# Weight pairs of two projections asked for by ScalarE behind a cast, in place of SyncE behind a gemv load

## The chip, the cores and the metric

The kernel runs on one core of a Trainium2 chip. A core has TensorE (PE in the profile; its weight loads are listed as PEld), VectorE (DVE), ScalarE (ACT), GpSimd (POOL) and SyncE (SP), each with a queue of instructions of its own that it works through in order. They share an on-chip memory (SBUF, 128 partitions) and the matmul banks (PSUM, eight banks of 128 x 512 floats). Data come from the chip's main memory by DMA: an engine's queue asks for a transfer, and 16 DMA engines move it. The metric is the device time of one execution in microseconds (us), lower is better.

## The reference

One decoder block on 512 tokens of width 2048, all in float32:

```python
mod = silu(c) @ w_ada + b_ada                      # six vectors of 2048
shift1, scale1, gate1, shift2, scale2, gate2 = split(mod, 6)
h = rms_norm(x, norm1_w) * (1 + scale1) + shift1
proj = h @ w_in                                    # 2048 x 7168
aq, ak, av, gq, gf, gi, gg = split(proj, ...)      # 1024 columns each
attn = rms_norm(dilated_attention(rope(rms_norm(aq)), rope(rms_norm(ak)), av), attn_out_norm_w)
hg = rms_norm(hgrn2(gq, gf, gi), hg_norm_w) * silu(gg)
x = x + gate1 * (concat([attn, hg]) @ w_out)       # 2048 x 2048
h2 = rms_norm(x, norm2_w) * (1 + scale2) + shift2
x = x + gate2 * (square(relu(h2 @ w_ff1)) @ w_ff2) # 2048 x 8192 x 2048
```

The attention has 8 heads of 128 with three dilated windows, merged by their softmax denominators; `hgrn2` is a gated linear recurrence with 8 heads of 128.

## The kernel before

**Split operands.** Every large product is made of three matmuls. An operand is split into a rounded part `hi` and a rest `lo = x - hi`, and `hi*hi + hi*lo + lo*hi` is summed in a bank. For weights this is `_split` (line 35): ScalarE casts the loaded tile to `whi` (line 39), and VectorE subtracts to get `wlo` (line 40). Both tiles have four buffers, so the cast of a row block waits until TensorE is done with the row block four places back.

**Loading weights.** `load_w` (line 188) loads a *pair*: two row blocks of 128 x 512, 512 KB in one DMA, into a tile `wraw` with four buffers, and splits both. A buffer is free when both casts and both splits of the pair four places back are done. The DMA is asked for on SyncE's queue (line 192). `load_w` runs under `tc.high_priority()`, which lets the planner place these instructions ahead of others.

**The projections.** `project` (line 371) makes 512 columns of `proj`: four banks, eight pairs, and for each row block twelve matmuls by `tok_mm` (lines 201 to 203) or `ch_mm` (209 to 211). After each row block it takes steps of other work: `tick()` advances the attention and recurrence tasks, `bg_step()` the gemv work. It is called eleven times after the first two column groups, which `first_groups` makes. `project_out` (line 877) makes 512 columns of the output projection in the same way and is called four times. Between two calls ScalarE copies the four banks out (lines 410, 570, 711, 944), since the next call needs banks too.

**The gemv.** The six modulation vectors are products of a single row, made on VectorE: `gemv` (line 118) loads `w_ada` piece by piece into `araw` (four buffers, 256 KB each, line 125, on SyncE's queue), and VectorE multiplies and adds (lines 129 and 131). `asked[0]` keeps the last such load. The results go through TensorE transposes (lines 151 and 182) and ScalarE (line 154).

**The order.** From line 849 on, the order of TensorE's instructions is the order in which the program is written. The order on the other engines and on SyncE's queue is set beforehand by a planner, which simulates the kernel with its own durations and priorities. `tc.issue_after(ins)` makes the instructions in its block come after `ins` on the same engine, without waiting for its end. In `project`, `marks` keeps for each pair the gemv load that was last asked for, and from the fourth pair on a weight pair comes behind the gemv load noted three pairs before. `project_out` has no such order.

**After the projections**, the feed-forward layer uses `load_w` without an order (lines 975 and 1013) and then larger weight tiles (line 1155) on SyncE's queue.

Of the kernel before, what the change touches and what calls it, by code (L numbers as in the profile page):

```python
# [34 lines left out]
def _split(nc, pool, src, n=512, eng=None):  # L35

    hi = pool.tile([P, 512], F32R, name="whi", tag="whi")[:, 0:n]
    lo = pool.tile([P, 512], F32R, name="wlo", tag="wlo")[:, 0:n]
    nc.scalar.copy(hi, src)  # L39
    (eng or nc.vector).tensor_tensor(lo, src, hi.bitcast(F32), op=ALU.subtract)  # L40
    return hi, lo

# [2 lines left out]
def hybrid_block(ctx, tc, x, c, positions, norm1_w, w_ada, b_ada, w_in, q_norm_w, k_norm_w,  # L45
                 attn_out_norm_w, hg_lb_logits, hg_norm_w, w_out, norm2_w, w_ff1, w_ff2,
                 lnc, hgmask, inv_freq, out):
    nc = tc.nc
    pe, dve, act, pool = nc.tensor, nc.vector, nc.scalar, nc.gpsimd
# [4 lines left out]
    win_v = w_in[0].rearrange("(k p) n -> p k n", p=P)  # L54
    wout_v = w_out[0].rearrange("(k p) n -> p k n", p=P)
# [5 lines left out]
    wr = pw.enter_context(tc.tile_pool(name="wr", bufs=4))  # L61
# [6 lines left out]
    def bank(name, tag="bg"):  # L68
        return ps.tile([P, 512], F32, name=name, tag=tag)
# [43 lines left out]
    pool.dma_start(ifq, inv_freq.broadcast_to([P, 16]))  # L113


    asked, marks = [None], []

    def gemv(view, vec, col0, n=512, early=False):

        accs = [(work("acc") if early else gv.tile([P, 512], F32, name="acc"))[:, 0:n] for _ in range(2)]  # L120
        nk = 512 // n
        for k0 in range(0, NK, nk):
            raw = spare.pop(0) if early and spare else slot("araw") if early else gv.tile([P, 512], F32, name="araw", bufs=4)
            raw = raw.rearrange("p (k n) -> p k n", n=n)
            asked[0] = nc.sync.dma_start(raw, view[:, k0:k0 + nk, col0:col0 + n])
            for k in range(k0, k0 + nk):
                acc = accs[k % 2]
                if k < 2:
                    dve.tensor_scalar(acc, raw[:, k - k0], vec[:, k:k + 1], None, op0=ALU.mult)
                else:  # L130
                    dve.scalar_tensor_tensor(acc, raw[:, k - k0], vec[:, k:k + 1], acc, op0=ALU.mult, op1=ALU.add)  # L131
            yield
        gemv.acc = accs
# [28 lines left out]
    def mod_cols(kind, b, dst, nw, n=512, early=False):  # L162

        for _ in gemv(ada_v, sc, kind * D + b * n, n, early):
            yield
        nb = n // P
        d = dst[:, b * nb:(b + 1) * nb]
        yield from to_cols(gemv.acc, d)
        dve.tensor_tensor(d, d, bcol[:, kind * NK + b * nb:kind * NK + (b + 1) * nb], op=ALU.add)
        if nw is not None:  # L170
            mod_cols.last = dve.scalar_tensor_tensor(d, d, 1.0, nw[:, b * nb:(b + 1) * nb], op0=ALU.add, op1=ALU.mult)
        yield
# [15 lines left out]
    def load_w(view, k0, c0, n=512, eng=None, ahead=True, raws=None, behind=False):  # L188
        with tc.high_priority() if ahead else ExitStack():
            raw = wr.tile([P, 2, n], F32, name="wraw", tag="raw", bufs=4)  # L190
            with tc.issue_after(marks[-3].ins) if behind else ExitStack():
                nc.sync.dma_start(raw, view[:, k0:k0 + 2, c0:c0 + n])
            if raws is not None:
                raws[:] = [raw[:, 0], raw[:, 1]]
            return [_split(nc, wr, raw[:, j], n, eng if j else None) for j in range(2)]

    def tok_mm(banks, hi, lo, whi, wlo, first, last):

        for ti in range(NT):
            ts = slice(ti * P, (ti + 1) * P)  # L200
            pe.matmul(banks[ti], lhsT=hi[:, ts], rhs=whi, start=first, stop=False)  # L201
            pe.matmul(banks[ti], lhsT=hi[:, ts], rhs=wlo, start=False, stop=False)  # L202
            pe.matmul(banks[ti], lhsT=lo[:, ts], rhs=whi, start=False, stop=last)  # L203
# [27 lines left out]
    def slot(name, dt=F32):  # L231
        return io.tile([P, 512], dt, name=name, tag="io")

    def work(name, dt=F32):
        return wk.tile([P, 512], dt, name=name, tag="wk")
# [55 lines left out]
    def first_groups(c_f, c_q, before, after):  # L291

        bt = [bank("prj", tag="mm") for _ in range(4)]
        bc = [bank("prc") for _ in range(2)]
        for k0 in range(0, NK, 2):
            before(k0)
            wt = load_w(win_v, k0, c_f, ahead=False)
            wc = load_w(win_v, k0, c_q, 256, None, ahead=False)
            for j in range(2):
                k = k0 + j  # L300
                ch_mm(bt, hhi[k], hlo[k], *wt[j], k == 0, k == NK - 1)
                ch_mm(bc, hhi[k], hlo[k], *wc[j], k == 0, k == NK - 1)
            after(k0)
        return bt, bc
# [14 lines left out]
    shift_done, behind = set(), []  # L319
# [29 lines left out]
    def bg_step():  # L349

        while bgw:
            try:
                return next(bgw[0])
            except StopIteration:
                bgw.pop(0)
# [3 lines left out]
    def tick(n=1):  # L359

        for _ in range(n):
            while tasks:
                try:
                    next(tasks[0])
                    break
                except StopIteration:
                    tasks.pop(0)
# [3 lines left out]
    def project(c0, mm, rate=1.85, after=None):  # L371

        banks = [bank("prj", tag="mm") for _ in range(4)]
        for k0 in range(0, NK, 2):
            for j, (whi, wlo) in enumerate(load_w(win_v, k0, c0, 512, None, behind=len(marks) > 2)):
                k = k0 + j
                mm(banks, hhi[k], hlo[k], whi, wlo, k == 0, k == NK - 1)
                tick()
                owed[0] += rate
                while owed[0] >= 1.0:  # L380
                    bg_step()
                    owed[0] -= 1.0
                if after:
                    after(k)
            marks.append(asked[0])
        return banks

    mix = [None] * NK
# [1 line left out]
    korder = list(range(8, 12)) + list(range(8)) + list(range(12, 16))  # L390

    def split_mix():

        if len(mixp) == NK or mix[korder[len(mixp)]] is None:
            return False
        mixp.append(pair(len(mixp)))
        split_to(mixp[-1], mix[korder[len(mixp) - 1]])
        return True
# [43 lines left out]
    def qk(c0, name, i):  # L442
        ts = evac(project(c0, tok_mm), name)
        rs = sm.tile([P, NT, 4], F32, name=f"rs{i}", bufs=2)
        bgw.insert(0, qk_norm(ts, i, rs))
        return ts if i else (ts, rs)
# [307 lines left out]
    def shift_through(col0):  # L754

        yield from gemv(win_v, s1c, col0, early=col0 < 4096 + 512)
        col = sm.tile([P, 8], F32, name="scol", bufs=2)
        yield from to_cols(gemv.acc, col[:, 0:4])
        for h in range(4):
            if col0 == 3072:  # L760
                dve.tensor_scalar(col[:, 4 + h:5 + h], col[:, h:h + 1], QS, None, op0=ALU.mult)
                sg = wk.tile([P, 512], F32, name="sg", tag="ev", bufs=2)
                act.activation(sg, hq0[h], AF.Sigmoid, scale=1.0 / QS, bias=col[:, h:h + 1])
                dve.scalar_tensor_tensor(hq0[h], hq0[h], col[:, 4 + h:5 + h], sg, op0=ALU.add, op1=ALU.mult)
            else:
                f, hd = ((f0, h), (f1, 4 + h))[(col0 - 4096) // 512]
                forget(hd, f[h], f[h], col[:, h:h + 1])
        yield
# [108 lines left out]
    def project_out(q, rate, after):  # L877
        banks = [bank("prj", tag="bg" if q % 2 and i < 2 else "mm") for i in range(4)]
        for i0 in range(0, NK, 2):
            for j, (whi, wlo) in enumerate(load_w(wout_v, korder[i0], q * 512)):  # L880
                i = i0 + j
                while q == 0 and len(mixp) <= i:
                    if not split_mix():
                        tick()
                while q == 0 and split_mix():
                    pass
                tok_mm(banks, *mixp[i], whi, wlo, i == 0, i == NK - 1)
                tick(2 if q == 0 and i < 10 else 1)
                owed[0] += rate
                while owed[0] >= 1.0:  # L890
                    bg_step()
                    owed[0] -= 1.0
                after(i)
        return banks
# [365 lines left out]
    def after(cs):  # L1260

        return {1: cs[5], 5: cs[6], 6: cs[1], 7: cs[7]}
# [78 lines left out]
    for item, following in zip(items, items[1:] + [None]):  # L1341
        stage_, blk, j, i = item
# [3 lines left out]
        if item == (2, (0, 0), 0, 1):  # L1346
# [3 lines left out]
            late = ctx.enter_context(tc.tile_pool(name="late", bufs=1, side="right", reuse_waits="tile"))  # L1350
# [17 lines left out]
        else:  # L1368
            q, c = blk
# [69 lines left out]
```

## Time and profile before

| what | value |
|---|---|
| time, median of 3 runs | 2274.01 us (2273.53 to 2277.32) |
| time of the profiled execution | 2273.89 us |
| its span, first to last instruction | 2272.1 us |
| wraw<-in_w_in, DMAs on SyncE's queue | 104 of 512 KB, 16 of 256 KB |
| wraw<-in_w_out, DMAs on SyncE's queue | 32 of 512 KB |
| araw<-in_w_ada, DMAs on SyncE's queue | 384 of 256 KB |
| data moved by SyncE's queue (q1) | 332.54 MB, 43.6% of the DMA engines' span |
| data moved by ScalarE's queue (q10) | 9.44 MB, 1.2% |

How to read the lines: `L192` is line 192 of the kernel; `wraw<-in_w_in_dram` names what is written and what is read; `SPq` and `ACTq` are DMA asks on SyncE's and ScalarE's queues. In the timeline each row has its start and length in us, the engine, the line, the operation and how many are merged (x3); in brackets stands the idle time of the engine before it and what ended it. In a view of waits each row has who waited for whom, the sum in us, the number of waits, and the longest. Matmuls are pipelined, so two rows of PE may overlap.

### The profile page before, as it was taken

The numbers are of one execution on the slowest core, as the hardware profiler recorded it, in microseconds if no ns is written. First come the engines' busy times: TensorE is split into PE (matmuls) and PEld (weight loads), VectorE is DVE, ScalarE is ACT, GpSimd is POOL, SyncE is SP. The second block draws the span as 40 slices with busy tenths as digits, with TensorE's granted clock in tenths as the row PEclk, the third lists the DMA queues.
The fourth block names the chain that finished last, engine by engine and source line by source line (L and its number), as shares of the span: only waits on it lengthen the run. The fifth ranks groups of instructions, "written<-read, shape, count | busy, mean of one in ns | idle before, by whom it ended". The sixth has DMA issues, their size and how long they took to land.

```text
span 2272.1 us, 33110 instructions
## 1 busy us (share of the span) xinstructions
PE 2219.7 (98%) x11769; PEld 1821.1 (80%) x11769; DVE 1809.6 (80%) x2765; ACT 1097.3 (48%) x1950; POOL 441.8 (19%) x664
## 2 busy tenths in 40 slices
PE   4899999999999999999999999999999999999999
PEld 3788778888778888888887888888888888888887
DVE  6999878768786575678658988998897779967878
ACT  5555434443454464457544555565564333443332
POOL 1000022000220000003232323323232222222221
PEclk9999999999999999999999999999999999999999
DMA  9799454646555266747879789879889987998884
GB/s 324 255 335 336 139 177 150 214 149 211 170 178 160 71 227 202 267 120 264 322 280 361 274 306 385 297 290 377 319 294 378 358 310 263 349 347 310 305 295 164
DMA packets 262583, 598.32 MB, mean 263 GB/s; under 512 B 23220, under 2 KB 43968, under 8 KB 262416
## 3 DMA queue, kind: packets, MB, share of 16 engines
q1 hardware_dynamic: 186800, 332.54, 43.6%
q0 software_dynamic: 70720, 254.21, 30.4%
q10 hardware_dynamic: 4896, 9.44, 1.2%
q8 instruction: 93, 1.52, 0.3%
q14 instruction: 74, 0.61, 0.1%
HBM read 518.49 MB, written 77.61 MB: 262 GB/s over the span
## 4 chain that ended last, share of the span: by engine, by line
PE 70%; DMA 10%; DVE 8%; issue 8%; POOL 2%; ACT 1%; SPq 0%; POOLq 0%; DVEq 0%; ACTq 0%
PE f L1197 9%; PE f L1196 9%; PE f L1195 9%; PE prj L201 8%; PE prj L203 8%; PE prj L202 8%; DMA araw<-in_w_ada_dram 3%; PE f L211 2%; PE f L209 2%; PE f L210 2%; DVE vlo L1180 2%; DMA f_lod<-fs 2%; DVE raw L1163 2%; PE prj L209 1%; PE prj L210 1%
## 5 line engine op out<-in xcount | busy, mean ns | idle before, releaser
L1179 ACT CAST vhi<-raw 128x1024 fp32r<-128x1024 f32 x392 | 413.5, 1055 | 534.1 <-PE f L1197 419.4
L1180 DVE TENSOR_TENSOR vlo<-raw,vhi 128x1024 fp32r<-128x1024 f32 x392 | 476.3, 1221 | 150.8 <-ACT vhi L1179 150.0
L1196 PE MATMUL f<-vlo,Fh 128*128 128x512 f32 x1376 | 537.1, 390 | 3.4 <-DVE vlo L1180 3.3
L1197 PE MATMUL f<-vhi,Fl 128*128 128x512 f32 x1376 | 535.8, 389 | 0.5 <-DMA Fl<-f_lod 0.5
L1195 PE MATMUL f<-vhi,Fh 128*128 128x512 f32 x1376 | 536.1, 390 | 0.0
L39 ACT CAST whi<-wraw 128x512 fp32r<-128x512 f32 (+1 forms) x368 | 219.8, 601 | 445.9 <-PE prj L203 309.7
L201 PE MATMUL prj<-whi,hi 128*128 128x512 f32 x896 | 363.5, 406 | 1.3 <-ACT gg L711 1.3
L203 PE MATMUL prj<-whi,lo 128*128 128x512 f32 x896 | 350.6, 391 | 0.0
L202 PE MATMUL prj<-wlo,hi 128*128 128x512 f32 x896 | 350.0, 391 | 0.6 <-DVE wlo L40 0.6
L40 DVE TENSOR_TENSOR wlo<-wraw,whi 128x512 fp32r<-128x512 f32 (+1 forms) x368 | 243.3, 666 | 115.3 <-ACT whi L39 109.5
L131 DVE SCALAR_TENSOR_TENSOR acc<-araw,sc,acc 128x512 f32<-128x512 f32 (+1 forms) x392 | 254.0, 674 | 99.8 <-DMA araw<-in_w_ada_dram 98.6
L1196 PEld LDWEIGHTS f<-vlo,Fh 128*128 128x128 f32 x1376 | 258.3, 188 | 62.3 <-DVE vlo L1180 8.9
L1197 PEld LDWEIGHTS f<-vhi,Fl 128*128 128x128 f32 x1376 | 258.3, 188 | 54.2 <-DMA Fl<-f_lod 0.9
L1195 PEld LDWEIGHTS f<-vhi,Fh 128*128 128x128 f32 x1376 | 258.3, 188 | 53.7
L1163 DVE TENSOR_TENSOR raw<-raw,raw 128x1024 f32<-128x1024 f32 x224 | 268.3, 1218 | 3.5 <-DMA raw<-in_w_ff_dram 3.1
L203 PEld LDWEIGHTS prj<-whi,lo 128*128 128x128 f32 x896 | 168.1, 188 | 36.6 <-DVE lo L243 0.3
L201 PEld LDWEIGHTS prj<-whi,hi 128*128 128x128 f32 x896 | 168.3, 188 | 36.4 <-ACT gg L711 1.6
L202 PEld LDWEIGHTS prj<-wlo,hi 128*128 128x128 f32 x896 | 168.6, 188 | 33.5 <-DVE wlo L40 1.7
L1141 POOL DMA_DIRECT2D Fh<-f_hid x112 | 79.0, 705 | 424.0 <-PE f L1197 410.3
L211 PE MATMUL f<-hi,wlo 128*128 128x512 f32 x256 | 99.9, 390 | 1.2 <-DVE wlo L40 1.2
L209 PE MATMUL f<-hi,whi 128*128 128x512 f32 x256 | 100.3, 392 | 0.0
L210 PE MATMUL f<-lo,whi 128*128 128x512 f32 x256 | 99.6, 389 | 0.0
(311 smaller groups left out, 2912.0 us busy)
## 6 DMA issues: line engine op xcount, KB each, us to landing
raw<-in_w_ff_dram SPq DMA_DIRECT2D x224, 512.0 KB, 10.1
araw<-in_w_ada_dram SPq DMA_DIRECT2D x384, 256.0 KB, 4.3
Fh<-f_hid POOLq DMA_DIRECT2D x112, 512.0 KB, 6.7
Fl<-f_lod POOLq DMA_DIRECT2D x112, 512.0 KB, 7.8
wraw<-in_w_in_dram SPq DMA_DIRECT2D x104, 512.0 KB, 4.4
Fh<-h_hid POOLq DMA_DIRECT2D x60, 512.0 KB, 6.4
Fl<-h_lod POOLq DMA_DIRECT2D x60, 512.0 KB, 7.4
f_hid<-part POOLq DMA_DIRECT2D x48, 512.0 KB, 8.0
```

What stands on the lines that cost most here:

```text
L39: nc.scalar.copy(hi, src)
L40: (eng or nc.vector).tensor_tensor(lo, src, hi.bitcast(F32), op=ALU.subtract)
L131: dve.scalar_tensor_tensor(acc, raw[:, k - k0], vec[:, k:k + 1], acc, op0=ALU.mult, op1=ALU.add)
L201: pe.matmul(banks[ti], lhsT=hi[:, ts], rhs=whi, start=first, stop=False)
L202: pe.matmul(banks[ti], lhsT=hi[:, ts], rhs=wlo, start=False, stop=False)
L203: pe.matmul(banks[ti], lhsT=lo[:, ts], rhs=whi, start=False, stop=last)
L1163: dve.tensor_tensor(dst, a, b, op=ALU.subtract)
L1179: cast_done.append(act.copy(hi, src))
L1180: split_done.append(dve.tensor_tensor(lo, src, hi.bitcast(F32), op=ALU.subtract))
L1195: pe.matmul(banks[t], lhsT=fh[u][a][:, ts], rhs=whi[:, a], start=first, stop=False)
L1196: pe.matmul(banks[t], lhsT=fh[u][a][:, ts], rhs=wlo[:, a], start=False, stop=False)
L1197: pe.matmul(banks[t], lhsT=fl[u][a][:, ts], rhs=whi[:, a], start=False, stop=end)
```

## The change

The order by `marks` goes, with the list and its entries. In its place `_split` leaves its cast as `_split.cast`, and `load_w` with `behind=True` keeps the cast of the second row block of each pair in the list `casts`. From the fourth such pair on, the DMA is asked for on ScalarE's queue, after the cast kept three pairs back. `project` and `project_out` both call it so. The first three pairs, the loads of `first_groups` and those of the feed-forward layer stay on SyncE's queue.

```diff
@@ _split
-    nc.scalar.copy(hi, src)
+    _split.cast = nc.scalar.copy(hi, src)
@@ hybrid_block
-    asked, marks = [None], []
+    casts = []
@@ gemv
-            asked[0] = nc.sync.dma_start(raw, view[:, k0:k0 + nk, col0:col0 + n])
+            nc.sync.dma_start(raw, view[:, k0:k0 + nk, col0:col0 + n])
@@ load_w
-            with tc.issue_after(marks[-3].ins) if behind else ExitStack():
-                nc.sync.dma_start(raw, view[:, k0:k0 + 2, c0:c0 + n])
+            late = behind and len(casts) > 2
+            with tc.issue_after(casts[-3].ins) if late else ExitStack():
+                (act if late else nc.sync).dma_start(raw, view[:, k0:k0 + 2, c0:c0 + n])
             if raws is not None:
                 raws[:] = [raw[:, 0], raw[:, 1]]
-            return [_split(nc, wr, raw[:, j], n, eng if j else None) for j in range(2)]
+            parts = [_split(nc, wr, raw[:, j], n, eng if j else None) for j in range(2)]
+            if behind:
+                casts.append(_split.cast)
+            return parts
@@ project
-            for j, (whi, wlo) in enumerate(load_w(win_v, k0, c0, 512, None, behind=len(marks) > 2)):
+            for j, (whi, wlo) in enumerate(load_w(win_v, k0, c0, 512, None, behind=True)):
...
-            marks.append(asked[0])
@@ project_out
-            for j, (whi, wlo) in enumerate(load_w(wout_v, korder[i0], q * 512)):
+            for j, (whi, wlo) in enumerate(load_w(wout_v, korder[i0], q * 512, behind=True)):
```

## The prediction, made before the changed kernel was run

> **What bounds the kernel now.** I read the page first, then the busy time by stage, then who waits for whom on TensorE, and only then the queue that the change relieves. The page:
>
> ```profile
> span 2272.1 us, 33110 instructions
> ...
> PE 2219.7 (98%) x11769; PEld 1821.1 (80%) x11769; DVE 1809.6 (80%) x2765; ACT 1097.3 (48%) x1950; POOL 441.8 (19%) x664
> ```
>
> TensorE is idle for 2272.1 - 2219.7 = 52.4 us. The change touches only the weight loads of `project` and `project_out`, whose matmuls lie between about 190 and 970 us. The windows view, by stage (busy us of PE, PEld, DVE, ACT, POOL, then granted clock, DMA share, GB/s):
>
> ```profile
> 0.00:190.00 190.00, 152.72 (x689) 123.52 (x689) 163.10 (x382) 106.04 (x243) 14.39 (x32) 0.98 0.92 310
> 190.00:970.00 780.00, 775.99 (x5301) 632.31 (x5301) 580.31 (x1225) 354.44 (x946) 74.00 (x123) 1.00 0.58 185
> ```
>
> Of the 52.4 us, 190.0 - 152.7 = 37.3 lie before the stage that the change touches, where the DMA engines are busy for 0.92. In the stage itself TensorE is idle for 780.0 - 776.0 = 4.0 us. The waits view of PE for that stretch names all of it:
>
> ```profile
> PE pr L182 <- DVE aq L509: 1.6, 1, 1.6
> PE prj L201 <- ACT gg L711: 1.3, 1, 1.3
> PE prj L202 <- DVE wlo L40: 0.6, 1, 0.6
> PE pc L151 <- DVE acc L145: 0.6, 1, 0.6
> ```
>
> Together 4.1 us. None of the four waits for a weight DMA. So TensorE bounds this stage, in an order that is written out by hand from line 849 on and does not move. Whatever is gained upstream is worth at most 4.1 us there, 0.18% of the time.
>
> **What SP loses today.** The waits view of SP's queue and of VectorE, same stretch:
>
> ```profile
> SPq L192 <- DVE wlo L40: 159.9, 68, 11.0
> SPq L125 <- DVE acc L131: 117.4, 167, 2.4
> ...
> SPq L192 <- DVE z L610: 64.0, 16, 6.8
> ...
> DVE acc L131 <- DMA araw<-in_w_ada_dram: 95.9, 75, 6.1
> ```
>
> SP stands for 159.9 us in front of a weight pair whose buffer VectorE has not yet split (L40), and I count the 64.0 us that the view puts down to L610 as the same kind. The gemv loads (`araw`, L125) stand behind it. VectorE in turn waits 95.9 us for `araw`. That is what the change can relieve. VectorE is not the bound, though: it is busy 580.3 of 780 us, and it counts only where TensorE waits for it.
>
> **Part 1: the weight asks leave SP.** The two functions load 11 x 8 + 4 x 8 = 120 pairs; the first three stay on SP, and 117 go to ScalarE. I follow the largest wait of the four, the one that ends at 443.5 us. Timeline, SP and VectorE:
>
> ```profile
> 431.76 3.89 SPq L125 DMA_DIRECT2D araw<-in_w_ada_dram  x5
> 435.92 0.38 SPq L192 DMA_DIRECT2D wraw<-in_w_in_dram  x1
> 436.58 7.88 SPq L125 DMA_DIRECT2D araw<-in_w_ada_dram  x6
> ...
> 435.20 0.69 DVE L40 TENSOR_TENSOR wlo<-wraw,whi 128x512 fp32r<-128x512 f32 x1
> ...
> 436.89 0.75 DVE L131 SCALAR_TENSOR_TENSOR acc<-araw,sc,acc 128x512 f32<-128x512 f32 x1 [0.34 <-DMA araw<-in_w_ada_dram]
> 438.53 0.75 DVE L131 SCALAR_TENSOR_TENSOR acc<-araw,sc,acc 128x512 f32<-128x512 f32 x1 [0.89 <-DMA araw<-in_w_ada_dram]
> 439.75 0.75 DVE L131 SCALAR_TENSOR_TENSOR acc<-araw,sc,acc 128x512 f32<-128x512 f32 x1 [0.47 <-DMA araw<-in_w_ada_dram]
> ...
> 441.66 0.75 DVE L131 SCALAR_TENSOR_TENSOR acc<-araw,sc,acc 128x512 f32<-128x512 f32 x1 [0.55 <-DMA araw<-in_w_ada_dram]
> 442.33 1.12 DVE L509 TENSOR_SCALAR aq<-po,lsum 128x128 f32<-128x128 f32 x4
> ```
>
> VectorE loses 0.34 + 0.89 + 0.47 + 0.55 = 2.25 us to `araw` just ahead of the L509 for which TensorE waits 1.6 us. How much of this is the weight pair's fault? SP's last gemv ask of the first group ends at 431.76 + 3.89 = 435.65. The weight pair goes when its split ends, 435.20 + 0.69 = 435.89, and is out at 435.92 + 0.38 = 436.30. So the pair holds SP for 436.30 - 435.65 = 0.65 us. The rest of the gap belongs to the gemv's own four buffers: the next six asks take 7.88 us without a weight pair among them. What is late next is VectorE's own row of L131s, which stand ahead of L509 whether they wait or not. I book 0.6 of the 1.6 us (bounds 0 and 1.6; 0.65 is the nearest row). The two waits of 0.6 also end in VectorE: I book half of each, 0.3 and 0.3 (bounds 0 and 0.6 each). The wait for `gg` ends in a copy on ScalarE, which no SP ask holds up: 0. The gain is 0.6 + 0.3 + 0.3 = 1.2 us, between 0 and 4.1.
>
> [...]
>
> **Part 2: ScalarE asks.** What an ask costs there is seen in the residual's `xin` loads, which ScalarE already issues (tile view, and the timeline of one):
>
> ```profile
> L956 ACTq DMA_DIRECT2D xin<-in_x_dram x16: 334/335/439, 837.0 to 953.1; - x16
> ...
> 837.95 0.62 ACT L39 CAST whi<-wraw 128x512 fp32r<-128x512 f32 x1 [2.35 <-PE prj L203]
> 837.98 1.55 ACTq L956 DMA_DIRECT2D xin<-in_x_dram  x2
> ...
> ACT whi L39 <- PE prj L203: 303.7, 151, 6.5
> ```
>
> The ask of 837.98 runs beside the cast of 837.95. So 117 asks of 0.335 us, 39 us in all, lie beside the casts that they follow, or in the 303.7 us in which ScalarE waits for TensorE before a cast. I cost them at nothing. Without that cover, one ask ahead of an urgent copy costs 0.34 us.
>
> **Part 3: the new wait.** An ask can go only when the buffer's last readers are done: the cast and the split of the pair four places back. On SP that wait held the gemv. On ScalarE it would hold every later instruction: casts, exponentials and the evacuations of the banks (L410, L711). The trace does not have this wait, so I laid the pairs side by side: the end of the cast three places back, and the end of the split four places back. First, longest and last case in which the split is later:
>
> ```profile
> 188.94 1.27 ACT L39 CAST whi<-wraw 128x512 fp32r<-128x512 f32 x2
> 191.09 0.69 DVE L40 TENSOR_TENSOR wlo<-wraw,whi 128x512 fp32r<-128x512 f32 x1
> ...
> 634.03 0.62 ACT L39 CAST whi<-wraw 128x512 fp32r<-128x512 f32 x1 [0.43 <-PE prj L203]
> 636.90 0.68 DVE L40 TENSOR_TENSOR wlo<-wraw,whi 128x512 fp32r<-128x512 f32 x1
> ...
> 955.99 0.62 ACT L39 CAST whi<-wraw 128x512 fp32r<-128x512 f32 x1
> 956.38 0.69 DVE L40 TENSOR_TENSOR wlo<-wraw,whi 128x512 fp32r<-128x512 f32 x1
> ```
>
> The holds are 191.78 - 190.21 = 1.57, 637.58 - 634.65 = 2.93 and 957.07 - 956.61 = 0.46 us. Over 116 pairs there are 10 such cases, 16.9 us in sum, 1.7 on average; in the other 106 the split is done before the cast ends. A hold costs something only where TensorE waits for ScalarE soon after. I compared the fifteen evacuations of banks with the matmul that needs the bank next. In five the room is under 0.2 us; the first and the last:
>
> ```profile
> 291.69 0.57 ACT L410 COPY aq<-prj 128x512 f32<-128x512 f32 x1
> 292.31 0.50 PE L201 MATMUL prj<-whi,hi 128*128 128x512 f32 x1
> ...
> 800.21 2.04 ACT L711 COPY gg<-prj 128x512 f32<-128x512 f32 x4
> 800.84 0.50 PE L201 MATMUL prj<-whi,hi 128*128 128x512 f32 x1 [1.33 <-ACT gg L711]
> ```
>
> A copy ends at 292.26 and the matmul starts at 292.31: a hold there goes straight to the end of the kernel. If holds fall as in the rows, 10 of 116, on the one ask near each of five tight places, the cost is 5 x 10/116 x 1.7 = 0.7 us (an estimate; bounds 0 and 16.9). A later arrival of the weights costs nothing. The pair behind the cast of 634.03 is cast at 652.32 us, 17.7 us after that cast's end at 634.65, and a pair lands in a few:
>
> ```profile
> wraw<-in_w_in_dram SPq DMA_DIRECT2D x84, 512.0 KB, 4.2
> ...
> 652.32 0.62 ACT L39 CAST whi<-wraw 128x512 fp32r<-128x512 f32 x1 [0.99 <-PE prj L203]
> ```
>
> **Part 4: dropping `marks`.** The NoSync order behind a gemv load of three pairs ago goes. It adds no instruction; its cover is that the cast now sets the pace. 0.
>
> **The sum.** -1.2 + 0.7 = -0.5 us. The profiled execution took 2273.89 us (2272.1 of span and 1.8 around it), the median of the runs is 2274.01; both minus 0.5 give 2273.4 and 2273.5. I say **2273.5 us**. A measurement of this kernel tells about 0.2% from no change, 4.5 us, so "faster" begins below 2269.5 and "slower" above 2278.5.
>
> **Rivals.** (a) *Faster*: all four waits go, -4.1: 2269.9, still within 0.2%. It needs something from the rest too, since the planner lays out everything behind the change anew. After 970 us the two largest waits of PE are:
>
> ```profile
> PE f L1196 <- DVE vlo L1180: 3.3, 6, 1.5
> PE f L211 <- DVE wlo L40: 1.2, 2, 0.7
> ```
>
> All gone too, the time is 2274.0 - 4.1 - 4.5 = 2265.4; a third of the extra 4.5 gives 2268.4. For it: VectorE's 95.9 us of waiting. Against it: the gemv's own buffers hold SP for 117.4 us, and these stay. Chance 0.12.
>
> (b) *Slower*: the asks hold ScalarE in front of the evacuations, so the wait for `gg` grows and the one at 292 appears. Each hold is 1.7 us; from three on tight places (3 x 1.7 = 5.1) it decides. Between three and five such holds make 5.1 to 8.5, some 2280 us; all ten holds, 16.9, would make 2291. For it: the ScalarE order is fixed by a plan made beforehand, and VectorE's real lateness (2.93 us above) is not in that plan. Against it: 106 of 116 asks find the buffer free, and at 291.69 the next cast, with its ask, follows the last copy. Chance 0.16. [...] No row of before shows a cast held behind a waiting ask.
>
> (c) *Nothing moves*: SP's loss was slack, and TensorE's four waits stay: 2274.0. It is told from my forecast by the waits alone, and shares its side.
>
> **Chances.** My forecast with (c): 0.72 (0.45 and 0.27), its own range 2270 to 2278; (a) 0.12; (b) 0.16. So faster 0.12, same 0.72, slower 0.16. The range of 8 in 10 reaches into both rivals, 2268.5 to 2280, and leaves out the far halves.
>
> **What would show it.** Right: on the page the weight rows of section 6 stand under ACTq, SP's waits at L192 in 190 to 970 us are gone but for the first pairs, VectorE's 95.9 us for `araw` is smaller, TensorE's idle time there stays under 6 us, and q10 carries the weights. Part 1 is wrong if the wait at L182 stays 1.6 us. Part 3 is wrong if TensorE waits at L201 or L209 for ScalarE copies over 3 us in sum, or if casts (L39) start late behind an ask. The whole is wrong if the first 190 us or the stage after 970 us change by more than 3 us: then the planner's new order, not the queue, made the time.

## The result, and the profile after

The changed kernel took 2281.43 us (median of 9 runs, 2280.24 to 2284.51), the kernel before 2275.96 us beside it (9 runs, 2273.53 to 2279.98). The ratio is 1.0029, with a 95% interval from 1.0021 to 1.0038: slower by about 6.6 us. The forecast was 2273.5 us, and the range ended at 2280.

The page of the changed kernel: the span, the engines' busy time, the two DMA queues, and the weights of `project` on ScalarE's queue.

```profile
span 2279.7 us, 33069 instructions
...
PE 2222.2 (97%) x11769; PEld 1824.0 (80%) x11769; DVE 1809.0 (79%) x2765; ACT 1096.7 (48%) x1950; POOL 440.4 (19%) x664
...
q1 hardware_dynamic: 154976, 271.19, 34.6%
...
q10 hardware_dynamic: 36720, 70.79, 9.8%
...
wraw<-in_w_in_dram ACTq DMA_DIRECT2D x85, 512.0 KB, 4.0
```

The span grew by 2279.7 - 2272.1 = 7.6 us. TensorE's idle time grew from 52.4 to 2279.7 - 2222.2 = 57.5 us, which is 5.1 of it; the other 2.5 are busy time, though the 11769 matmuls are the same. Some of them ran slower. The windows by stage (busy us of PE, PEld, DVE, ACT, POOL, granted clock, DMA share, GB/s) and TensorE's waits from 190 to 970 us say where:

```profile
0.00:190.00 190.00, 154.06 (x694) 124.58 (x695) 164.41 (x384) 107.24 (x245) 14.40 (x32) 0.98 0.92 313
190.00:970.00 780.00, 769.29 (x5254) 626.92 (x5254) 573.45 (x1215) 348.06 (x935) 72.55 (x123) 1.00 0.57 183
970.00:2280.00 1310.00, 1298.86 (x5824) 1072.51 (x5822) 1071.10 (x1169) 641.43 (x770) 353.47 (x509) 1.00 0.83 302
```

```profile
PE pB L586 <- DVE z L613: 4.1, 3, 2.7
PE pr L182 <- DVE aq L512: 2.4, 1, 2.4
PE pho L694 <- ACT far_sb L686: 2.1, 1, 2.1
PE prj L205 <- ACT gg L714: 1.3, 1, 1.3
PE pc L151 <- DVE acc L145: 0.7, 1, 0.7
```

Idle time in the stage went from 4.0 to 780.0 - 769.3 = 10.7 us. The first 190 us became 1.3 us better (35.9 idle, not 37.3), and the rest stayed as it was. Line numbers are four higher than before in the first part of the kernel, three higher later: L586, L613 and L686 are L583, L610 and L683 of before. Two waits are new (z, pho), the one at `pr` has grown from 1.6 to 2.4 us, the one for `gg` is the same, and that for `wlo` is gone.

**The wait for `z`**, an operand of the recurrence, is the largest: 2.66 of its 4.1 us come at once, at 340.3 us. VectorE makes `z` (L613) shortly behind a multiplication of the gemv, and that one waits for its load. SyncE asks for this load at 332.92 us, right behind a pair that ScalarE asks for at 332.53; the pair lands at 337.32 and the load at 337.96. Rows of ScalarE's and VectorE's timelines, and behind them VectorE's row at the same place before:

```profile
332.53 0.37 ACTq L193 DMA_DIRECT2D wraw<-in_w_in_dram  x1
...
338.05 0.75 DVE L131 SCALAR_TENSOR_TENSOR acc<-araw,sc,acc 128x512 f32<-128x512 f32 x1 [3.77 <-DMA araw<-in_w_ada_dram]
...
339.86 0.42 DVE L613 TENSOR_TENSOR z<-gq,f 128x256 f32<-128x256 f32 x1
```

```profile
334.48 0.75 DVE L131 SCALAR_TENSOR_TENSOR acc<-araw,sc,acc 128x512 f32<-128x512 f32 x1 [2.43 <-DMA araw<-in_w_ada_dram]
```

VectorE waited there before too, 2.43 us, and TensorE did not have to wait. This is read from the two traces; no run moved that one load.

**What the slow matmuls are.** The windows view around two of these waits, same columns:

```profile
440.00:447.50 7.50, 5.18 (x32) 3.92 (x30) 4.78 (x11) 0.62 (x1) 0.00 (x0) 1.00 0.73 243
447.50:453.00 5.50, 5.40 (x18) 4.28 (x19) 5.50 (x13) 0.87 (x2) 0.00 (x0) 0.69 0.59 181
453.00:460.00 7.00, 7.00 (x32) 5.80 (x31) 3.90 (x11) 3.34 (x10) 0.00 (x0) 1.00 0.67 184
...
649.20:653.60 4.40, 4.27 (x19) 3.92 (x20) 4.40 (x11) 4.40 (x16) 0.00 (x0) 0.61 0.73 223
653.60:660.00 6.40, 6.40 (x90) 5.10 (x89) 3.89 (x9) 3.19 (x12) 0.00 (x0) 1.00 0.52 144
```

The granted clock is 0.69 and 0.61 in windows that begin right behind the waits for `pr` and `pho`, and 1.00 next to them. A matmul's start laid beside that of the same matmul of before gives the price: the delay grows by 0.9 us at the wait for `pr` and by another 1.56 in the slow matmuls up to 452.0; by 2.3 at `pho` and by another 1.7 up to 653.5. So the wait of 2.13 us at `pho` costs 4.0. The three waits for `z` add 4.3 us without slow matmuls. That makes 10.8 us; TensorE was 1.1 us ahead when the first of them came, and on balance gets back 1.8 us after 938 us.

**What moved at `pho`.** ScalarE's timeline, first before, then after:

```profile
637.21 0.62 ACT L39 CAST whi<-wraw 128x512 fp32r<-128x512 f32 x1 [2.29 <-PE prj L203]
638.20 0.59 ACT L683 COPY far_sb<-pE 128x512 f32<-128x512 f32 x1 [0.37 <-PE pE L682]
643.19 2.16 ACT L439 ACTIVATE ak<-ak,rs 128x128 f32<-128x128 f32 x7 [4.40 <-POOL rs L215]
```

```profile
639.76 0.62 ACT L39 CAST whi<-wraw 128x512 fp32r<-128x512 f32 x1 [0.44 <-PE prj L207]
642.53 0.37 ACTq L193 DMA_DIRECT2D wraw<-in_w_in_dram  x1
642.94 0.37 ACT L680 COPY far_sb<-pD 128x256 f32<-128x256 f32 x1 [2.56 <-PE prj L207]
643.30 0.62 ACT L39 CAST whi<-wraw 128x512 fp32r<-128x512 f32 x1
648.12 0.69 ACT L442 ACTIVATE ak<-ak,rs 128x128 f32<-128x128 f32 x2 [4.20 <-POOL rs L219]
648.72 0.56 ACT L686 COPY far_sb<-pE 128x512 f32<-128x512 f32 x1
```

Before, the copy `far_sb<-pE`, which TensorE needs, stands ahead of the `ak` normalisations, which wait over 4 us for GpSimd. Afterwards it stands behind two of them. The diff does not touch either line: the planner has laid out the kernel anew. Some 90 of VectorE's 2765 instructions and some 15 of ScalarE's 1667 (without DMAs and table loads) stand elsewhere, the exact number depending on how moves are counted, and four of TensorE's transposes; SyncE's other loads and GpSimd's instructions keep their order. So two things changed at once, the queue of the weights and the order of all other work, and the experiments take them apart.

### The profile page after: what moved, and what is told of

Same layout as the page of the kernel before. It is cut to its first block, busy times and chain, and to the rows that moved or that the text cites. A ratio compares the mean times of both kernels' runs of the same rounds, so it can differ in the third digit from the quotient of the medians.

```text
span 2279.7 us, 33069 instructions
## 1 busy us (share of the span) xinstructions
PE 2222.2 (97%) x11769; PEld 1824.0 (80%) x11769; DVE 1809.0 (79%) x2765; ACT 1096.7 (48%) x1950; POOL 440.4 (19%) x664
## 4 chain that ended last, share of the span: by engine, by line
PE 62%; DMA 12%; DVE 11%; issue 10%; POOL 3%; ACT 1%; SPq 0%; POOLq 0%; DVEq 0%; ACTq 0%
PE f L1199 9%; PE f L1200 9%; PE f L1198 9%; PE prj L205 6%; PE prj L207 6%; PE prj L206 6%; DMA araw<-in_w_ada_dram 6%; DMA f_lod<-fs 2%; PE f L215 2%; PE f L214 2%; PE f L213 2%; DVE acc L131 2%; DVE vlo L1183 2%; DMA f_hid<-part 1%; PE prj L213 1%
```

## The experiments

In the *pinned* kernels the planner is given an order: the names of the instructions of VectorE, ScalarE and TensorE (the same in both kernels, but for two of VectorE's) are listed in the order of one kernel, and each is put behind the one ahead of it on its engine. This adds no wait; DMA asks stay where the planner puts them. That pinning costs nothing measurable by itself is seen in all_sp below, which is pinned and takes the time of before.

```diff
@@ _program
         hybrid_block(tc, *args)
+        _pin(tc)
@@ _pin
+    by = {i.name: i for i in tc.nc.cur_bb.bb.instructions}
+    for names in _PLAN:
+        for a, b in zip(names, names[1:]):
+            tc.add_manual_dep(by[b], a, mybir.DependencyInfo(mybir.DependencyClass.NoSync,
+                                                             mybir.DependencyReason.DATA), reason="plan")
```

### Queue and order apart

q_new_p_old is the changed kernel in the order of before; q_old_p_new is the kernel before in the order of the changed one.

> The changed kernel, with the order of VectorE's, ScalarE's and TensorE's instructions pinned to that of before; only the 117 weight asks stand on ScalarE's queue. Theory P (the planner's new order made the loss): 2272 to 2277 us, no wait of TensorE over 1 us at the pB and pho matmuls, the wait before pr back at about 1.6 us. Theory Q (the asks on ScalarE's queue made it, by sharing the DMA engines with the gemv loads or by holding ScalarE): 2280 to 2283 us, with the waits at pB still there.

Measured: 2277.72 us (11 runs), ratio 1.0018 [1.0009, 1.0027]. This lies between the two theories; the waits at `pho` and, but for 0.5 us, at `pB` are gone, as P says, and `pr` is at 1.9 us.

> The kernel before, weight asks on SyncE's queue behind the gemv loads, with the order of VectorE's, ScalarE's and TensorE's instructions pinned to that of the changed kernel. Theory P: 2280 to 2283 us, with the waits at pB, pho and pr of the changed kernel. Theory Q: 2273 to 2277 us.

Measured: 2284.50 us (5 runs), ratio 1.0043 [1.0029, 1.0056]. This is above theory P's range, and far above Q's.

Both parts cost by themselves, some 4.5 us and 11 us against 2273.22 of before on that chip, and together they cost less than their sum. The order is the larger one: with the old queue, TensorE's waits from 190 to 1260 us are these.

```profile
PE f L211 <- DVE wlo L40: 3.2, 2, 3.0
PE pr L182 <- DVE aq L509: 2.4, 1, 2.4
PE pt L1225 <- DVE s L1244: 2.2, 2, 2.0
PE pho L691 <- ACT far_sb L683: 2.1, 1, 2.1
```

The waits at `pr` and `pho` are those of the changed kernel, with no weight ask on ScalarE. Waits are only part of the 11 us: TensorE's busy time is 2224.7 us, 5.0 more than before, and three stretches of low clock stand behind the waits at `pr`, `wlo` and `pt` (a transpose after the projections). The wait at `z` is 0.7 us here and 4.1 in the changed kernel. In the five traces with a new order and the weights of `project` on ScalarE it is 2.0 to 4.1 us in sum, in the other nine at most 0.8, so a long one needs both. With the new queue and the old order, the time goes at another place, early in the stage. First TensorE's waits from 190 to 260 us, then VectorE's from 196 to 222, then ScalarE's timeline:

```profile
PE prj L206 <- DVE wlo L40: 2.9, 2, 1.6
```

```profile
DVE s1c L169 <- ACT pc L154: 3.5, 1, 3.5
```

```profile
201.78 0.61 ACT L39 CAST whi<-wraw 128x512 fp32r<-128x512 f32 x1
205.43 0.37 ACTq L193 DMA_DIRECT2D wraw<-in_w_in_dram  x1
205.85 0.26 ACT L154 ACTIVATE pc<-pc 128x128 f32<-128x128 f32 x1 [3.46 <-DMA araw<-in_w_in_dram]
```

The ask waits, and behind it on ScalarE stands the copy L154, which makes the gemv result `s1c`. VectorE waits 3.5 us for that, its splits come late, and TensorE waits twice for `wlo`. ScalarE is held by an ask, as Part 3 feared, but ahead of a gemv result and not of a bank's evacuation, and most of the hold is not for the split that Part 3 counted: the last split ahead of it ends at 203.12 us, and the ask goes at 205.43, just behind the landing at 205.35 of a gemv load. The last section says which load that is.

### One function at a time

The change in `project` alone, then in `project_out` alone, the planner free in both:

```diff
@@ in_only, against the changed kernel: project_out
-            for j, (whi, wlo) in enumerate(load_w(wout_v, korder[i0], q * 512, behind=True)):
+            for j, (whi, wlo) in enumerate(load_w(wout_v, korder[i0], q * 512)):
@@ out_only, against the kernel before: load_w
-            with tc.issue_after(marks[-3].ins) if behind else ExitStack():
-                nc.sync.dma_start(raw, view[:, k0:k0 + 2, c0:c0 + n])
+            late = act_q and len(casts) > 2
+            with tc.issue_after(casts[-3].ins) if late else tc.issue_after(marks[-3].ins) if behind else ExitStack():
+                (act if late else nc.sync).dma_start(raw, view[:, k0:k0 + 2, c0:c0 + n])
@@ out_only: project_out
-            for j, (whi, wlo) in enumerate(load_w(wout_v, korder[i0], q * 512)):
+            for j, (whi, wlo) in enumerate(load_w(wout_v, korder[i0], q * 512, act_q=True)):
```

> The change in project alone; project_out asks on SyncE's queue as before. The changed kernel loses 10.7 us against before between 200 and 655 us and gets 2.4 back after 900 us. If the loss belongs to project and the gain to project_out: 2282 to 2286 us, slower than the changed kernel. Theory P alone allows anything, since the plan differs again: 2272 to 2286 us.

Measured: 2282.52 us (5 runs), ratio 1.0035 [1.0023, 1.0048], inside both ranges.

> The change in project_out alone; project as before, on SyncE's queue behind the gemv loads. If the gain after 900 us belongs to the queue of project_out: 2271 to 2274 us, about 2 us faster than before, the wait at L202 for the split near 938 us gone. If it belongs to the plan: as before within 2 us.

Measured: 2272.14 us (11 runs), ratio 0.9994 [0.9985, 1.0003]. The wait for `wlo` stays, at 0.5 us.

All of the loss comes with `project`. In `project_out` the asks on ScalarE neither gain nor lose anything that can be measured. As the planner was free, this alone does not tell the queue from the order.

### The order by engine, and one copy in it

far_first is the changed kernel pinned to its own order, but for the copy `far_sb<-pE`, which stands ahead of the two `ak` normalisations again. plan_act and plan_dve are the kernel before with half of the new order each: ScalarE's, or VectorE's and TensorE's.

```diff
@@ far_first: ScalarE's list
-  cast, ak, ak, far_sb<-pE, ak
+  cast, far_sb<-pE, ak, ak, ak
```

> The changed kernel in its own order on VectorE, ScalarE and TensorE, except that one copy on ScalarE, far_sb<-pE (L686), stands ahead of the two ak normalisations (L442) that it followed. Theory A, that this place in the order costs what the trace shows there (TensorE waits 2.1 us at pho L694, and then its granted clock is low for about 3.4 us, which cost 1.4 us): 2281.4 - 3.5 = 2278, and the wait at pho is gone. Theory B, that TensorE only meets the next late instruction there (the ask for the weights that ScalarE waits 2.5 us for at 642.5): over 2280, with another TensorE wait between 640 and 660 us.

Measured: 2278.72 us (11 runs), ratio 1.0018 [1.0009, 1.0026]; before took 2273.70 beside it. TensorE's waits from 630 to 1020 us:

```profile
PE f L215 <- DVE wlo L40: 2.6, 1, 2.6
PE prj L205 <- ACT gg L714: 1.3, 1, 1.3
```

Theory A holds for the place: the wait at `pho` is gone, and the slow matmuls behind it too (matmul by matmul 2.3 and 1.7 us). But the span only fell from 2279.7 to 2277.6. At 1004.7 us TensorE, now early, meets a `wlo` that VectorE makes too late, waits 2.6 us, and runs slowly behind it. Ahead of this place TensorE is 6.3 us earlier than in the changed kernel, but that split only 2.2 us (it starts at 1003.95 and 1006.10), so there the delay upstream had hidden it. (Not all of the 6.3 us comes from the copy: the waits for `z` happen to be 2.0 us in sum in this trace, not 4.1.) What is left of the gain lies within the intervals of the two ratios (1.0029 and 1.0018).

> The kernel before, weights on SyncE's queue, with the order of VectorE and TensorE pinned to its own and the order of ScalarE to that of the changed kernel. The whole new order cost 11 us on the old queue. Theory A, ScalarE's 16 moved instructions carry most of it: 2278 to 2285, with the wait at pho for far_sb of 2 us and a stretch of low clock behind it. Theory B, VectorE's 95 carry it: 2272 to 2278, so that of the new order on ScalarE only the wait at pho is left (2 to 4 us).

Measured: 2278.16 us (11 runs), ratio 1.0019 [1.0010, 1.0028]. This is where the two ranges meet.

> The kernel before, weights on SyncE's queue, with the order of VectorE and TensorE pinned to that of the changed kernel and the order of ScalarE to its own. Theory A (ScalarE's order carries the loss): within 3 us of before, 2271 to 2276. Theory B (VectorE's order carries it): 2278 to 2285, with TensorE's wait at pr L182 over 2 us, at wlo L40 near 1007 us over 2.5 us, and a stretch of low clock behind each.

Measured: 2279.21 us (11 runs), ratio 1.0021 [1.0012, 1.0029], in theory B's range. Only `pr` has low clock behind it in the profiled run, `wlo` has not.

Neither theory of the two holds alone: the engines share the loss, some 4.5 and 5.5 of 11 us. The waits from 190 to 1260 us name the places, ScalarE's order first and VectorE's second:

```profile
PE pho L691 <- ACT far_sb L683: 2.4, 1, 2.4
```

```profile
PE f L211 <- DVE wlo L40: 3.5, 2, 2.8
PE pr L182 <- DVE aq L509: 3.1, 1, 3.1
```

For ScalarE the one copy is most of it: beside its wait of 2.4 us TensorE's busy time is 1.4 us longer than before, with a stretch of low clock behind that wait. For VectorE the two waits are seen and the single instruction behind them was not tried.

### The early asks, and marks

In five kernels the first eleven pairs, or all of them, stay on SyncE's queue: the bound on `len(casts)` is raised.

```diff
@@ load_w, in hv0_sp, hv0_new and hv0_free
-            late = behind and len(casts) > 2
+            late = behind and len(casts) > 10
@@ load_w, in all_sp and all_sp_free
-            late = behind and len(casts) > 2
+            late = behind and len(casts) > 1000
```

hv0_sp is pinned to the order of before, hv0_new to that of the changed kernel, all_sp to that of before.

> The changed kernel with VectorE, ScalarE and TensorE pinned to the order of before, as in the run that gave 2277.7 us, but with the first eleven pairs on SyncE's queue, so that ScalarE asks only from about 230 us on. Theory A, the early asks hold ScalarE (3.5 us at 202 to 205.4 us, ahead of the copies L154 that the gemv result s1c needs) and TensorE pays for it with two waits of 1.6 us at wlo: both waits go, 2277.7 - 3.1 = 2274.6. Theory B, the loss comes from how the loads share the DMA engines: 2277 to 2278, and the waits stay or come back elsewhere.

Measured: 2274.01 us (11 runs), ratio 1.0006 [0.9996, 1.0015]. Theory A: the two waits for `wlo` at 214 and 218 us (2.9 us in sum) are gone, and of the 4.5 us above before 0.3 are left against the 2273.70 beside it (1.4 by the ratio). With 109 pairs still asked for by ScalarE nothing remains that can be measured, though a longer hold than that of 205 us is among them (ScalarE's timeline):

```profile
634.04 0.62 ACT L39 CAST whi<-wraw 128x512 fp32r<-128x512 f32 x1 [0.42 <-PE prj L207]
638.42 0.37 ACTq L193 DMA_DIRECT2D wraw<-in_w_in_dram  x1
638.84 0.37 ACT L680 COPY far_sb<-pD 128x256 f32<-128x256 f32 x1 [4.17 <-DVE z L610]
```

The ask keeps the copy `far_sb<-pD` for 4.2 us, and TensorE does not wait for that copy.

> The changed kernel pinned to its own order on VectorE, ScalarE and TensorE, with the first eleven pairs on SyncE's queue. Theory A, the planner's new order was laid around the early asks, so that their holds (2.7 us at 203) cost TensorE nothing there: 2280 to 2282.5, as the changed kernel. Theory B, the early asks cost 3 to 4 us in any order: 2277 to 2278.5.

Measured: 2281.04 us (8 runs), ratio 1.0026 [1.0016, 1.0037]. Theory A again: in the new order, sparing the early asks gains nothing that can be measured (the changed kernel has 1.0029).

> The changed kernel's code with all weight pairs of the two functions on SyncE's queue and without the order behind gemv loads, VectorE, ScalarE and TensorE pinned to the order of before: what dropping marks does by itself. Theory A, marks held nothing that mattered: within 0.1% of before, 2272 to 2275, SyncE's order about as before. Theory B, without marks the weight pairs stand elsewhere in SyncE's queue and hold the gemv: over 2276, with TensorE waits for VectorE grown at L40 or L182.

Measured: 2274.43 us (11 runs), ratio 1.0004 [0.9995, 1.0014]. Dropping `marks` by itself changes nothing that can be measured; the interval runs from -1 to +3 us.

### Left to the planner

The same two codes with the planner free. Dropping `marks` alone moves some 70 instructions of VectorE and 5 of ScalarE; with the first eleven pairs on SyncE it is some 110 and 15.

> Dropping marks alone, all weight pairs on SyncE's queue, and the planner free: it moves 70 instructions of VectorE and 5 of ScalarE against before, but the copy far_sb<-pE stays ahead of the ak normalisations. With before's order this code took the time of before (1.0004). Theory A, a new order costs what it costs at single places, above all at the far_sb copy (some 4 us) and at pr L182: 2273 to 2278, no wait at pho, and a rise only as far as a wait at pr, z or wlo grows in the trace. Theory B, any order other than the old one costs about the same: 2279 or more.

Measured: 2273.41 us (11 runs), ratio 1.0006 [0.9998, 1.0015]. Theory A: a new order need not cost anything that can be measured. The copy `far_sb<-pE` keeps its place and nothing waits at `pho`. Some moved instructions do delay TensorE: in the profiled run (2275.21 us) it waits 2.2 us at `pr` and 2.0 at `pt`, each with low clock behind it.

> The changed kernel with the first eleven pairs on SyncE's queue and the planner free: it moves 112 instructions of VectorE and 16 of ScalarE, and the far_sb copy again stands behind two ak normalisations. Theory A (single places): a wait at pho of about 2 us with slow matmuls behind it, 2278 to 2284. Theory B (the early asks made the loss): 2272 to 2276.

Measured: 2281.15 us (5 runs, 2278.20 to 2282.39), ratio 1.0035 [1.0022, 1.0049]. Theory A: the copy stands behind the `ak` again, and the waits at `z`, `pho` and `pr` (190 to 1260 us) are back.

```profile
PE pB L586 <- DVE z L613: 2.4, 1, 2.4
PE pho L694 <- ACT far_sb L686: 2.2, 1, 2.2
PE pr L182 <- DVE aq L512: 2.1, 1, 2.1
```

All ratios side by side, each to the runs of before on the same chip:

| order of the engines | weights on SyncE | ScalarE from 230 us on | ScalarE from the fourth pair on |
|---|---|---|---|
| that of before | 1 (without marks 1.0004) | 1.0006 | 1.0018 |
| that of the changed kernel | 1.0043 | 1.0026 | 1.0029 |
| the planner's own for each | 1 (without marks 1.0006) | 1.0035 | 1.0029 |

None of these kernels is measurably faster than the one before.

## Why the prediction was wrong

**The step that failed is the sum.** "-1.2 + 0.7 = -0.5 us" was made in before's trace, as if the other engines kept their order and only the queue of the weights moved. It has no term for the planner's new order. Part 4, "It adds no instruction; its cover is that the cast now sets the pace. 0", is right for what it names: dropping `marks` by itself is worth 0 as far as can be measured (1.0004). But the change as a whole made the planner lay out VectorE and ScalarE anew, and that costs 11 us with the old queue. With the weights asked for by ScalarE from 230 us on, the new order has 1.0026 [1.0016, 1.0037] and the old one 1.0006 [0.9996, 1.0015]. With all asks from the fourth pair on it is 1.0029 against 1.0018, and these intervals overlap. The prediction knew of this: rival (a) says that the planner lays out everything behind the change anew, and counts it only as a gain; the last sentence gives it as the thing that would break the whole, and looks for it in the wrong stages. The first 190 us and the part after 970 us hardly changed. It struck inside the stage. The prediction also says that TensorE's order "does not move"; four transposes near 197 us did. What was missing is a rival with a place and a price, such as an urgent copy that falls behind instructions that wait over 4 us for GpSimd.

Even without the new order the sum is off: with the order of before, the new queue costs 1.0018 [1.0009, 1.0027], 2 to 6 us, where -0.5 was forecast. Most of what the trace shows of it, 2.9 us, belongs to Part 3.

**Part 1 failed by itself.** It booked 0.6 us of the wait at `pr` L182 as gain; the wait grew to 2.4. SyncE was relieved as forecast: from 190 to 970 us no weight pair is left among its waits. But VectorE's wait for `araw` did not shrink, and the gemv loads became late all the same. VectorE's waits in the stage, and the timeline of SyncE, ScalarE and VectorE ahead of L512:

```profile
DVE acc L131 <- DMA araw<-in_w_ada_dram: 99.2, 70, 4.2
```

```profile
435.47 11.39 SPq L125 DMA_DIRECT2D araw<-in_w_ada_dram  x10
...
436.99 0.37 ACTq L193 DMA_DIRECT2D wraw<-in_w_in_dram  x1
...
443.17 1.42 DVE L131 SCALAR_TENSOR_TENSOR acc<-araw,sc,acc 128x512 f32<-128x512 f32 x2 [2.72 <-DMA araw<-in_w_ada_dram]
```

The view of line 125 gives the time from ask to landing, here of the gemv loads asked for from 435 to 437 us, from 437.5 to 441 and from 443 to 446:

```profile
DMA to landing us min/median/max: 2.5/2.6/2.7
DMA to landing us min/median/max: 4.5/5.2/5.3
DMA to landing us min/median/max: 2.6/2.6/2.8
```

SyncE asks for ten gemv loads in a row, with no pair among them. ScalarE asks for a pair at 436.99, and the four loads behind it land after a median of 5.2 us, not 2.6. So the pair delays the gemv through ScalarE's queue too. It is not the whole of the wait at `pr`: in the order of before the new queue makes it 1.9 and 2.0 us (q_new_p_old, hv0_sp), and the new order on the old queue makes it 2.4 with no pair on ScalarE (q_old_p_new), so the order is the larger part of its growth. With all pairs on SyncE's queue and `marks` gone it was 1.8 (all_sp). These are single traces. No run with weights on ScalarE's queue is measurably faster than before (the lowest ratio is 0.9994 [0.9985, 1.0003], in out_only).

**Part 2 held.** The asks cost nothing measurable by their length: 109 of them, from 230 us on, have 1.0006 [0.9996, 1.0015].

**Part 3 had half of the mechanism, and not the place.** "An ask can go only when the buffer's last readers are done" leaves out a second condition: the ask also waits for the landing of the load that used its semaphore before (last section). It counted 10 holds of 16.9 us in sum. In the changed kernel ten asks start over 0.75 us behind the start of the ScalarE instruction ahead of them, 18.7 us beyond the usual 0.3. Seven of them go 0.03 us behind the end of a split, as Part 3 says; one is the ask of 642.53 shown above. Three, among them that of 202.96, go 0.08 us behind a landing. So that the number and the sum agree is in part luck. The waits at the evacuations stayed as forecast: `gg` 1.3 us, none at 292 us. What it missed is L154 near 205 us, a short chain through the gemv, held by a landing. In the order of before this costs the two waits of 2.9 us in sum, and with the first eleven pairs on SyncE they are gone; Part 3 had booked 0.7 us for all holds. In the planner's new order, laid out with the ask in its place, it costs nothing that can be measured. In q_new_p_old the 3.46 us ahead of L154 show the ask's wait holding the instruction behind it on ScalarE.

**The rivals.** The time came out where (b) put it, near 2280, but not by (b)'s mechanism: the evacuations were not held, so that number is luck. (a) and (c) are out. Of the five signs for being right, three came (the weights under ACTq and on q10, SyncE's waits at L192 gone) and two did not: VectorE's wait for `araw` is 99.2 us, not under 95.9, and TensorE's idle time in the stage is 10.7, not under 6.

**A term that was in no part**: the slow matmuls behind a wait, 1.6 and 1.7 us in the profiled run, where TensorE's busy time is 2.5 us longer in all. They are not peculiar to that run: the mean granted clock of the changed kernel's nine runs is 0.996 or 0.997, and 0.998 in 72 of the 87 runs of before for which it is on record.

## What to carry to other kernels

Where a planner orders the engines, a change of a queue is two changes. Price the new order as a rival of its own, with the tightest copy or split as its place, and pin the old order to measure the queue alone. Another queue for a load did not take it out of the way of other loads here (a median of 5.2 us from ask to landing behind a pair on ScalarE's queue, not 2.6). Look at everything that an ask waits for before it goes on a queue with urgent work behind it: here one held L154 for 3.46 us (q_new_p_old). And a wait that is removed upstream can come back further down, where an engine's order had room only because TensorE was late: in far_first 2.6 us at 1004.7 us.

## What the runs showed of the hardware

**The clock after short waits.** The two waits of 2.42 and 2.13 us were each followed by a stretch of 3.41 us at a granted clock of 0.50 (448.7 to 452.1 and 650.0 to 653.5). Not every such wait was: behind the wait of 2.66 us for `z` at 340.3 us in the changed kernel the windows view shows full clock.

```profile
340.30:344.00 3.70, 3.67 (x46) 3.09 (x47) 2.91 (x9) 0.23 (x1) 0.00 (x0) 1.00 0.75 219
```

Between 110 and 2200 us, the fourteen traces have 26 waits of TensorE of 1.8 to 3.1 us. Sixteen were followed by a stretch at a granted clock of 0.5, each 3.41 us long; the shortest of these waits was 1.82 us, the longest without one 2.81. None of the 44 waits from 1.0 to 1.8 us was. The profiled run of hv0_free had its three waits of 2.1 to 2.4 us without any low clock, and was the fastest of its five runs by 2.7 us; the others have no trace, but three of the four show a mean granted clock of 0.997, and it 0.998. So waits of 1.82 to 3.13 us were enough here for a stretch of 3.41 us; what decides which of them is followed by one is not shown.

**An ask can wait for another load.** The early holds were longer than the split that frees the buffer explains. In the traces of before and of the changed kernel the 915 asks of SyncE and ScalarE use eight semaphores between them, 114 or 115 asks each, to tell of their landing, and none of the 907 asks whose semaphore had been used starts before the load that had it before has landed. So an ask can be held by the landing of an earlier load on either queue, most often the one asked for eight asks earlier (in before, 899 of the 907). In the changed kernel the split in question ends at 201.38 us, and the ask starts at 202.96, right behind the landing at 202.88 of the gemv load eight asks earlier; ahead of it, at 202.91 us, the sequencer has an instruction that waits for just this semaphore. In q_new_p_old the ask of 205.43 goes behind such a landing at 205.35. In before, 165 asks start within 0.15 us of such a landing. An instruction of the program makes this wait, so it belongs to the kernel as it was built; that the chip itself has such a limit is not shown, and no run varied the number of semaphores.
